# Attention units beside a projection: values, transposes and scores in one piece or in three

## The chip, the cores and the metric

The kernel runs on one core of a Trainium2 chip, as one program. The metric is the device time of an execution in microseconds, the median of several runs. Beside it there is one profiled execution, from which all durations come.

## What is computed

One decoder layer for a prompt of 1024 tokens and 8 single sampled tokens, all in fp32. The change lies in the prompt's attention, beside the input projection. The reference, cut to that:

```python
h = rms_norm(x, norm_mix_pre)
q, k, v, u, gates = jnp.split(h @ w_in, IN_SPLITS, axis=-1)
# three head groups of 4 heads x 64: (window, dilation) = (128,1), (512,4), (2048,16)
s = jnp.einsum('bnqrhd,bnkrhd->bnrhqk', qb, kw) * SCALE + bias
s = jnp.where(valid[None, :, None, None], s, NEG)
lse = jax.nn.logsumexp(s, axis=-1)
pr = jnp.exp(s - lse[..., None])
o = jnp.einsum('bnrhqk,bnkrhd->bnqrhd', pr, vw)
# the groups are combined with the softmax of their lse; then the attention output,
# a conformer convolution of u, gates, an output projection, a SwiGLU, an embedding
```

A block of 128 queries reads its own block of keys and, in the first group always but for the first block and in the second group for every other block, the block before. In the third group it reads its own block alone.

## The kernel before

**The projection.** The activations lie in SBUF with features on partitions, split into a high and a low part (`hh`, `hl`), as is each weight (`wh` on ScalarE, `wl` on VectorE, written by `ensure`). A bank of the projection (`gemm_bank`) is one PSUM bank of 384 or 264 tokens, into which 8 x 3 matmuls accumulate (L288 to L290: high x high, low x high, high x low). Each weight column block gives three banks, of 384, 384 and 264 tokens.

**The order of the work.** It is written out by hand in `CYCLES`: a triple (`triple(i)`: the q, k and v of two heads, 9 banks), then a pair (`u_pair`: gate and input of one block of the convolution, 6 banks), and so on, six of each. Then come the banks of the branch gates (`wi_gB`, `wi_gA`). After each bank `pump(BUD)` lets background generators go on, in their order: the depthwise convolution (30 operations of VectorE per block), the sampled tokens' attention, and `combine` with the layer norm. The program's instructions are then put in order for each engine by a scheduler that goes by this order and by what is ready, so that an instruction whose operand or buffer isn't free yet can be passed by later ones.

**A unit of attention** (`Unit`) is two query blocks of two heads (four blocks in the third group). It has three steps:

- `qk` (L645): scores of both heads into the PSUM banks `S0` and `S1`, from 64 rows each. VectorE adds the bias and takes the extreme, ScalarE exponentiates into two SBUF tiles `E`.
- `pt(i)` (L672): transposes of one half of the unit's `E`, 128x128 each, into the PSUM bank `PT`, and a copy by ScalarE to SBUF (`PTs`).
- `pv` (L690): values, `PTs` against the token-ordered v, into the PSUM bank `O`, 64 columns per head, and a copy by ScalarE to the output tile `oT`. After a triple's last unit `oT` is written to DRAM (`d_o`).

A triple of the first two groups has four units, one of the third two; there are 20 in all. They are queued when their triple's q, k and v are done (`triple_done`, after the first gate bank of the following pair) and run beside the banks that follow: `attn_slot` is called after each of the pair's three input banks, after each of the next triple's nine banks, and after the gate banks while units are left. When none is left there, `attn_done` gives the attention's PSUM banks to other work and queues `combine`.

**The slots before.** A unit takes two calls. In the first, `attn_slot` issues the values of the unit before and the scores of this one. In the second it issues `pt(0)` and leaves `pt(1)` in the list `mids`; the next bank calls it in its middle, ahead of its sixth of eight steps (`MID = 5`). So the projection is interrupted three times for each unit.

**The buffers in question.** `misc()` gives the next PSUM bank of a rotation; while units run it holds one bank alone, `m`. Other users of `m` there: the transpose of the sampled rows in `qkv_out` (L737), the first half of the transposes of v in `to_tok` (L764; the second half uses `PT`), and the transpose of the convolution's last rows (`rows`, L985), which runs at the end of the bank after a pair. The pool `sc` has four buffers, for `E`, `PTs` and the rows `nrow` and `zrow`. The pool `act` has 43 slots of 1032 columns, for q, k, v, outputs, split weights and the convolution's tiles.

Of the kernel before, what the change touches and what calls it, by code (L numbers as in the profile page):

```python
# [10 lines left out]
F32 = mybir.dt.float32  # L11
# [5 lines left out]
P = 128  # L17
# [41 lines left out]
def decoder_step(ctx: ExitStack, tc: tile.TileContext, ins, outs):  # L59
# [3 lines left out]
    def pool(name, bufs, space=None):  # L63
        if space is None:
            return ctx.enter_context(tc.tile_pool(name=name, bufs=bufs))
        return ctx.enter_context(tc.tile_pool(name=name, bufs=bufs, space=space))
# [9 lines left out]
    psa = pool("psa", 1, PSUM)  # L76
# [3 lines left out]
    def nm(s):  # L80
        uid[0] += 1
        return f"{s}_{uid[0]}"
# [4 lines left out]
    def sc(s, shape=(P, 512)):  # L87
        return scp.tile(list(shape), F32, tag="sc", name=nm(s))
# [14 lines left out]
    def misc():  # L103
        nonlocal mtags
        mtags.rotate(-1)
        return psa.tile([P, 512], F32, tag=mtags[-1], name=nm("m"))
# [185 lines left out]
    def gemm_bank(wi, xs, c, nk=KT, mid=None, at=MID):  # L292

        t0, n = rng(c)
        ps = bank()
        sp = W(wi)
        for k in range(nk):
            if k == at and mid is not None:
                mid()
            if k == MID and mids:  # L300
                mids.popleft()()
            xh, xl = xs[k]
            mm3(ps[:, :n], n, sp[0][:, k], sp[1][:, k],
                xh[:, t0:t0 + n], xl[:, t0:t0 + n], k == 0, k == nk - 1)
        while later:
            later.popleft()()
        return ps

    def gemm_bank_rows(wis, f, xs, c):

        t0, n = rng(c)
        ps = bank()
        nk = len(wis)
        for k in range(nk):
            xh, xl = xs[k]
            sp = W(wis[k])
            mm3(ps[:, :n], n, sp[0][:, f], sp[1][:, f],
                xh[:, t0:t0 + n], xl[:, t0:t0 + n], k == 0, k == nk - 1)
        return ps
# [104 lines left out]
    last = [j for j in range(NH) if all(j not in x for x in pairs)]  # L424
# [191 lines left out]
    class Unit:  # L616
# [46 lines left out]
                        A.activation(ev, ev, AF.Exp, scale=-1.0, bias=nm_, accum_out=l_)  # L663

        def pt(self, i):
            ps = psa.tile([P, 512], F32, tag="PT", name=nm("PT"))
            e, half = self.e[i], self.halves[i]
            for blk in half:
                for h in range(2):
                    for kb in range(0 if self.prev(blk) else 1, 2):  # L670
                        o = self.at(blk, h, kb)[1]
                        TE.transpose(ps[:, o:o + P], e[:, o:o + P], ident)  # L672
            self.p[i] = p = sc("PTs")
            if self.g == 2 or self.prev(half[0]):
                A.activation(p, ps, AF.Copy)
            else:
                A.activation(p.rearrange("p (h b q) -> p h b q", h=2, b=2)[:, :, 1],
                             ps.rearrange("p (h b q) -> p h b q", h=2, b=2)[:, :, 1], AF.Copy)
# [25 lines left out]
                    stats_by_tokens(g)  # L704

    steps = deque()
    flight = [None]
    mids = deque()

    def attn_slot():  # L710


        while mids:
            mids.popleft()()
        u = flight[0]
        if u is not None and u.p[0] is None:
            u.pt(0)
            mids.append(lambda: u.pt(1))
            return
        if u is not None:  # L720
            u.pv()
        flight[0] = steps.popleft() if steps else None
        if flight[0] is not None:
            flight[0].qk()

    def attn_busy():
        return bool(steps) or flight[0] is not None

    def attn_steps(g, hp, qT, kT, vtok, oT):
        steps.extend(Unit(g, hp, n, qT, kT, vtok, oT) for n in range(4 if g < 2 else 2))  # L730
# [269 lines left out]
    def u_pair(i):  # L1000
        sig, zs = {}, {}
        for c in range(3):
            ensure(wi_gate[i] + 1)
            u_banks(i, c, sig)
            if c == DONE and done:
                triple_done(done.pop())
            pump(BUD)
        for c in range(3):
            ensure(wi_a[i] + 1)
            a_banks(i, c, sig, zs)  # L1010
            attn_slot()
            pump(BUD)
# [73 lines left out]
    def triple(i):  # L1086
        for j in range(3):
            for c in (0, 2, 1) if i == 0 and j == 0 else range(3):
                ensure(wi_qkv[i, j] + 1)
                triple_bank(i, j, c)  # L1090
                attn_slot()
                pump(BUD)
        while attn_busy():
            attn_slot()
        done.append(i)
# [55 lines left out]
    for wis, dst in ((wi_gB, d_gB), (wi_gA, d_gA)):  # L1151
        for i in range(KT):
            for c in range(3):
                ensure(wis[i] + 1)
                t0, n = CH[c]
                ps = gemm_bank(wis[i], hs, c)
                s = rl("sg")
                A.activation(s[:, :n], ps[:, :n], AF.Sigmoid)
                SY.dma_start(dst[i, :, t0:t0 + n], s[:, :n])
                if attn_busy():  # L1160
                    attn_slot()
                elif rest:
                    rest.pop()()
                pump(BUD)
# [17 lines left out]
    for c in range(3):  # L1182
        t0, n = CH[c]
        for f in range(KT):
            ga = rl("ga")
            SY.dma_start(ga[:, :n], d_gA[f, :, t0:t0 + n])
            ps = gemm_bank_rows(wi_A, f, ohl, c)
# [675 lines left out]
```

## Time and profile before

| what | value |
|---|---|
| median of 3 runs | 1684.11 us (1683.31 to 1684.15) |
| profiled execution | 1686.02 us |
| its span, first to last instruction | 1684.2 us |
| mean granted clock of TensorE | 0.998 |
| TensorE matmuls busy | 1660.8 us, 99% of the span |
| VectorE busy | 1203.5 us, 71% |
| ScalarE busy | 670.2 us, 40% |
| GpSimd busy | 112.4 us, 7% |

How to read the rows of the profile: PE is TensorE's matmuls, PEld its weight loads, DVE is VectorE, ACT is ScalarE, POOL is GpSimd, SP issues transfers. A row of the timeline has the start in us from the span's start, the duration, engine, line, operation, output and inputs by name, the form (rows x columns of the array, then the moving operand) and the number of instructions merged. Matmuls overlap and their ends are modelled, so the time that one takes from the engine is read from start to start. L120 is the line of a helper through which all VectorE, ScalarE, GpSimd and SP instructions pass; those are told apart by their tiles. An fp32 matmul of scores or values appears as two instructions, a transpose as one. Rows of a waits view have the waiting instruction, what ended the wait, the sum in us, the number of times and the longest.

### The profile page before, as it was taken

Reading aid. Unit: us, or ns where it says so; the run is one execution under the profiler, and the core shown is the slowest. Engines: PE = TensorE matmul, PEld = TensorE weight load, DVE = VectorE, ACT = ScalarE, POOL = GpSimd, SP = SyncE. Lnnn points to the kernel's source line nnn. Section 1 sums busy time; section 2 is a strip of 40 time slices with the busy share of each in tenths; the row PEclk is TensorE's granted clock in tenths of the full one; section 3 lists DMA queues with packets and bytes.
Section 4 is the critical chain, followed back from the end, with each engine's and each line's share of the span. In section 5 each row is a group of like instructions: output and inputs, shape, how many; then the busy total and the mean of one; then the engine's idle time right before and its main releaser. Section 6 shows DMA issues by size and latency. Waiting matters only on the chain.

```text
span 1684.2 us, 29605 instructions
## 1 busy us (share of the span) xinstructions
PE 1660.8 (99%) x11843; PEld 1632.8 (97%) x11843; DVE 1203.5 (71%) x2156; ACT 670.2 (40%) x1419; POOL 112.4 (7%) x129
## 2 busy tenths in 40 slices
PE   7999999999999999999999999999999999999998
PEld 7999999999999999999999999999999999999998
DVE  7889879859979686644679666566678445668853
ACT  6434445444353345113445444344444341223520
POOL 1000000000000000000000000000000197200000
PEclk9999999999999999999999999999999999999999
DMA  5241121121355263522233245345445676740411
GB/s 192 65 126 61 49 68 39 55 90 56 102 163 171 85 192 121 160 81 87 92 116 113 97 164 187 140 176 201 169 150 194 238 253 229 254 143 14 156 54 47
DMA packets 103296, 217.00 MB, mean 129 GB/s; under 512 B 13074, under 2 KB 64098, under 8 KB 102774
## 3 DMA queue, kind: packets, MB, share of 16 engines
q1 hardware_dynamic: 102966, 214.97, 37.8%
q8 instruction: 93, 1.52, 0.4%
q0 software_dynamic: 192, 0.13, 0.1%
q14 instruction: 45, 0.37, 0.1%
HBM read 157.30 MB, written 71.26 MB: 136 GB/s over the span
## 4 chain that ended last, share of the span: by engine, by line
PE 91%; DVE 5%; ACT 1%; DMA 1%; issue 1%; POOL 0%; SPq 0%; POOLq 0%; DVEq 0%; ACTq 0%
PE g L288 29%; PE g L290 29%; PE g L289 29%; DVE y L120 3%; PE O L690 1%; PE S L645 1%; PE PT L672 1%; DVE wl L120 1%; DMA ux<-d_s 0%; PE m L347 0%; PE m L335 0%; DVE pk L120 0%; DMA strow<-in_state_conv_dram 0%; DVE ts L120 0%; DMA raw<-in_w_in_dram 0%
## 5 line engine op out<-in xcount | busy, mean ns | idle before, releaser
L288 PE MATMUL g<-hh,wh 128*128 128x384 f32 (+1 forms) x1200 | 393.5, 328 | 7.5 <-ACT wh L120 7.5
L290 PE MATMUL g<-hh,wl 128*128 128x384 f32 (+1 forms) x1200 | 384.8, 321 | 0.2 <-DVE wl L120 0.2
L289 PE MATMUL g<-hl,wh 128*128 128x384 f32 (+1 forms) x1200 | 384.3, 320 | 0.0
L120 DVE SCALAR_TENSOR_TENSOR y<-z,taps,y 128x1023 f32<-128x1023 f32 (+14 forms) x240 | 304.0, 1267 | 36.7 <-ACT y L120 31.1
L288 PEld LDWEIGHTS g<-hh,wh 128*128 128x128 f32 x1200 | 226.8, 189 | 14.8 <-ACT wh L120 7.5
L289 PEld LDWEIGHTS g<-hl,wh 128*128 128x128 f32 x1200 | 226.6, 189 | 0.6 <-DVE hl L120 0.3
L290 PEld LDWEIGHTS g<-hh,wl 128*128 128x128 f32 x1200 | 226.2, 188 | 0.8 <-DVE wl L120 0.8
L120 DVE TENSOR_TENSOR fa<-fa,g 128x258 f32<-128x258 f32 (+1 forms) x216 | 91.3, 433 | 84.2 <-PE g L290 72.7
L120 DVE TENSOR_TENSOR wl<-raw,wh 128x1024 fp32r<-128x1024 f32 x90 | 109.5, 1221 | 34.9 <-ACT wh L120 29.0
L288 PE MATMUL g<-mh,wh 128*128 128x344 f32 x336 | 108.0, 322 | 0.0
L290 PE MATMUL g<-mh,wl 128*128 128x344 f32 x336 | 107.4, 320 | 0.0
L289 PE MATMUL g<-ml,wh 128*128 128x344 f32 x336 | 107.3, 319 | 0.0
L120 ACT ACTIVATE wh<-raw 128x1024 fp32r<-128x1024 f32 x90 | 94.0, 1052 | 17.5 <-issue 7.7
L288 PE MATMUL g<-mh,wah 128*128 128x258 f32 x304 | 86.8, 287 | 5.5 <-DVE pk L120 5.5
L120 ACT ACTIVATE sg<-g 128x384 f32<-128x384 f32 (+1 forms) x68 | 31.0, 455 | 146.1 <-PE g L290 123.6
L289 PE MATMUL g<-ml,wah 128*128 128x258 f32 x304 | 87.0, 287 | 0.0
L290 PE MATMUL g<-mh,wal 128*128 128x258 f32 x304 | 86.9, 286 | 0.0
L288 PE MATMUL g<-th,wbh 128*128 128x258 f32 x304 | 86.4, 285 | 0.1
L289 PE MATMUL g<-tl,wbh 128*128 128x258 f32 x304 | 85.9, 283 | 0.0
L290 PE MATMUL g<-th,wbl 128*128 128x258 f32 x304 | 85.8, 283 | 0.0
L120 ACT ACTIVATE p<-g 128x258 f32<-128x258 f32 x114 | 42.6, 382 | 91.4 <-PE g L290 88.2
L120 DVE TENSOR_TENSOR acc<-acc,sq 128x344 f32<-128x344 f32 (+2 forms) x123 | 61.3, 512 | 17.6 <-ACT sq L120 15.2
(285 smaller groups left out, 4347.0 us busy)
## 6 DMA issues: line engine op xcount, KB each, us to landing
raw<-in_w_in_dram SPq DMA_DIRECT2D x50, 512.0 KB
raw<-in_w_ffn_in_dram SPq DMA_DIRECT2D x44, 512.0 KB
d_s<-tsh SPq DMA_DIRECT2D x16, 516.0 KB
d_s<-ts SPq DMA_DIRECT2D x16, 516.0 KB
ush<-d_s SPq DMA_DIRECT2D x16, 516.0 KB
usl<-d_s SPq DMA_DIRECT2D x16, 516.0 KB
raw<-in_w_ffn_out_dram SPq DMA_DIRECT2D x32, 256.0 KB
out_kvs_dram<-in_cache_kv_w_dram SPq DMA_DIRECT2D x16, 510.0 KB
```

The costliest lines, as they stand in the source:

```text
L120: ins = fn(*a, **k)
L288: TE.matmul(ps, hi_w, xh, start=first, stop=False, skip_group_check=more)
L289: TE.matmul(ps, hi_w, xl, start=False, stop=False, skip_group_check=more)
L290: TE.matmul(ps, lo_w, xh, start=False, stop=last, skip_group_check=more)
L645: TE.matmul(sp[h][:, o:o + nk], qT[h * 64:(h + 1) * 64, blk * P:(blk + 1) * P], kT[h * 64:(h + 1) * 64, (blk + 1) * P - nk:(blk + 1) * P], ...
L672: TE.transpose(ps[:, o:o + P], e[:, o:o + P], ident)
L690: TE.matmul(ps[h * 64:(h + 1) * 64, i * P:(i + 1) * P], vtok[:, k0:k0 + 64], self.p[half][:, o:o + P], start=kb == kbs[0], stop=kb == kbs[-1])
```

## The change

A unit now interrupts the projection once in every second call of `attn_slot`; the calls between return at once. In one piece it issues the values of unit k-1, both halves of the transposes of unit k and the scores of unit k+1. So a unit's scores, transposes and values lie two calls apart each, and three units are under way. The second half of the transposes takes its PSUM bank from `misc()` instead of `PT`. Nothing is put into `mids` any more.

```diff
         def pt(self, i):
-            ps = psa.tile([P, 512], F32, tag="PT", name=nm("PT"))
+            ps = psa.tile([P, 512], F32, tag="PT", name=nm("PT")) if i == 0 else misc()
             e, half = self.e[i], self.halves[i]
...
     steps = deque()
-    flight = [None]
+    flight = [None, None]
     mids = deque()
+    turn = [0]
 
     def attn_slot():
 
 
-        while mids:
-            mids.popleft()()
-        u = flight[0]
-        if u is not None and u.p[0] is None:
+        turn[0] ^= 1
+        if not turn[0]:
+            return
+        last, u = flight
+        if last is not None:
+            last.pv()
+        if u is not None:
             u.pt(0)
-            mids.append(lambda: u.pt(1))
-            return
-        if u is not None:
-            u.pv()
-        flight[0] = steps.popleft() if steps else None
-        if flight[0] is not None:
-            flight[0].qk()
+            u.pt(1)
+        flight[:] = u, steps.popleft() if steps else None
+        if flight[1] is not None:
+            flight[1].qk()
 
     def attn_busy():
-        return bool(steps) or flight[0] is not None
+        return bool(steps) or any(u is not None for u in flight)
```

By the count of calls, twelve from one `triple_done` to the next, a triple's four units begin at the second call and end at the twelfth, where before they began at the first and ended at the ninth.

## The prediction

> **What bounds the kernel now.** I read the page first, its chain above all, then the busy times of the stretch in which attention runs, then the matmuls of TensorE one by one around single interruptions, and last the waits.
>
> ```profile
> span 1684.2 us, 29605 instructions
> ...
> PE 91%; DVE 5%; ACT 1%; DMA 1%; issue 1%; POOL 0%; SPq 0%; POOLq 0%; DVEq 0%; ACTq 0%
> ```
>
> The chain that ended last runs on TensorE for 91% of 1684.2 us. The units of attention lie between 100 and 480 us, and there the busy times are:
>
> ```profile
> 100.00:480.00 380.00, 379.71 (x2664) 361.46 (x2664) 329.11 (x462) 172.99 (x420) 4.60 (x6) 1.00 0.21 68
> ```
>
> TensorE is busy for 379.71 of 380.00 us, VectorE for 329.11 and ScalarE for 172.99, at full clock. So in this stretch what TensorE gains or loses is gained or lost by the kernel one for one, and a latency elsewhere counts only where TensorE comes to wait for it. The profiled execution took 1686.02 us, its span plus 1.8 us around it, and the runs have a median of 1684.11. I make the sum as a difference in the profiled execution and add it to the median.
>
> The question is what one interruption costs, beyond the matmuls that it must do anyway. I time it by starts: from the last projection matmul before to the second one after, less the usual step of these two.
>
> ```profile
> 213.38 0.34 PE L289 MATMUL g<-hl,wh 128*128 128x384 f32 x1
> 213.56 0.34 PE L290 MATMUL g<-hh,wl 128*128 128x384 f32 x1
> 213.73 0.60 PE L672 MATMUL PT<-ident,E 128*128 128x128 f32 x4
> 214.09 0.42 PE L288 MATMUL g<-hh,wh 128*128 128x384 f32 x1
> 214.34 0.34 PE L289 MATMUL g<-hl,wh 128*128 128x384 f32 x1
> ```
>
> A 384-wide matmul is followed by the next after 0.175 us (213.38 to 213.56). Four transposes: 214.34 - 213.56 - 2 x 0.175 = 0.43 us, 0.11 each. The third row starts at the usual step after the one before. The first matmul behind it is lengthened, to 0.25, but this is inside the 0.43. Scores and values are another matter:
>
> ```profile
> 254.98 0.34 PE L290 MATMUL g<-hh,wl 128*128 128x384 f32 x1
> 255.25 0.93 PE L645 MATMUL S<-kT,qT 64*128 64x128 f32 x8
> 256.10 0.45 PE L288 MATMUL g<-hh,wh 128*128 128x384 f32 x1
> 256.38 0.34 PE L289 MATMUL g<-hl,wh 128*128 128x384 f32 x1
> ```
>
> ```profile
> 294.02 0.29 PE L289 MATMUL g<-hl,wh 128*128 128x264 f32 x1
> 294.14 0.28 PE L290 MATMUL g<-hh,wl 128*128 128x264 f32 x1
> 294.35 0.88 PE L690 MATMUL O<-PTs,vtok 128*64 128x128 f32 x12
> 295.16 0.44 PE L288 MATMUL g<-hh,wh 128*128 128x384 f32 x1
> 295.44 0.34 PE L289 MATMUL g<-hl,wh 128*128 128x384 f32 x1
> ```
>
> ```profile
> 284.49 0.34 PE L290 MATMUL g<-hh,wl 128*128 128x384 f32 x1
> 284.75 0.88 PE L690 MATMUL O<-PTs,vtok 128*64 128x128 f32 x12
> 285.56 0.93 PE L645 MATMUL S<-kT,qT 64*128 64x128 f32 x8
> 286.42 0.44 PE L288 MATMUL g<-hh,wh 128*128 128x384 f32 x1
> 286.69 0.34 PE L289 MATMUL g<-hl,wh 128*128 128x384 f32 x1
> ```
>
> Scores alone cost 256.38 - 254.98 - 0.35 = 1.05. Both are of the second head group, the same size as in the third fence. Values alone cost 295.44 - 294.14 - 0.12 - 0.175 = 1.00, the step of a 264-wide matmul being 0.12 (294.02 to 294.14). Both in one piece cost 286.69 - 284.49 - 0.35 = 1.85, so 0.20 us less than apart. Where the form changes from 128*128 to 64*128 or 128*64 the next start comes late: 255.25 is 0.27 after 254.98, 0.09 over the step, and the second matmul behind the piece comes after 0.28, 0.10 over it. Transposes have the form of the projection, 128*128, and show no late start in front of them. This is the whole argument: what costs is not the interruption but the change of form, and the transposes don't change it.
>
> **The change part by part.**
>
> *Interruptions removed.* Two per unit, both made of transposes alone. At 0.43 us for four they cost the transposes' own 0.11 each and nothing besides, at a bank's end or in the middle of a bank. Taking them out of the projection saves 0.00 us; the same transposes are issued.
>
> *Transposes between values and scores.* Before, a triple of four units had the pieces S0, O0+S1, O1+S2, O2+S3, O3, with transposes in between. After, it has S0, T0+S1, O0+T1+S2, O1+T2+S3, O2+T3, O3. A triple of two units had S0, O0+S1, O1 and gets S0, T0+S1, O0+T1, O1. Values and scores stood side by side at 4 x 3 + 2 x 1 = 14 places, and after the change at none. The trace of before doesn't show transposes next to either. If they act there as the projection does, being of its form, each of the 14 places loses the 0.20: +2.8 us. If both borders of the transposes cost no more than the border of values and scores, the 14 borders O to T and the 14 borders T to S save 0.20 each against a pass over the projection, and the balance is -28 x 0.20 + 14 x 0.20 = -2.8 us. I take a value near the upper end, since the nearest row to a transpose is the projection's, the same 128*128. Part of the late start of scores (0.09) can run within the last transpose's 0.11, of which its 128 columns need not take all: I count a third, 0.03 x 14 = 0.4 off. That gives +2.4 us.
>
> The Trainium skill, page "TensorEngine Tiling (Array Packing)", section Key Properties, says that changing the tiling mode, and not just the tile, drains TensorE. It speaks against this change: O to T to S holds two changes of mode where O to S holds one. The trace agrees: late starts stand at the changes of form and nowhere else. By this rule alone each of the 14 pieces has one drain more and the sum lies above zero; the page has no figure for the drain.
>
> *Waits for the exponentials go.* Before, the transposes come one bank behind the scores; after, two.
>
> ```profile
> 396.49 0.34 PE L290 MATMUL g<-hh,wl 128*128 128x384 f32 x1
> 396.67 1.19 PE L672 MATMUL PT<-ident,E 128*128 128x128 f32 x4
> 397.61 0.37 PE L288 MATMUL g<-hh,wh 128*128 128x264 f32 x1
> 397.82 0.28 PE L289 MATMUL g<-hl,wh 128*128 128x264 f32 x1
> ```
>
> ```profile
> PEld PT L672 <- ACT E L120: 1.2, 5, 0.2
> PEld g L290 <- DVE wl L120: 1.1, 3, 0.8
> ```
>
> Here four transposes cost 397.82 - 396.49 - 0.175 - 0.12 = 1.03, 0.60 over their price: VectorE, deep in the convolution, was late with the softmax's maxima. The weight loader's waits for E add up to 1.2 us in five pieces, and a little more on the array: I take -1.3 us. What is late next is nothing on TensorE: the transposes come a bank later still, 24 x 0.12 = 2.9 us at least. If VectorE's delay grows as much, the 1.3 stay: bounds -1.3 to 0.
>
> *The second half's bank.* pt(1) writes "m" in place of "PT", so the two halves don't wait for each other's copy. Elsewhere this costs nothing; at the first unit of each triple "m" is just in use (second rival).
>
> *Held longer.* q and k of a triple live one bank longer, its token-ordered v and its output three. The 43 slots also hold split weights; VectorE's waits row above shows only 1.1 us of waiting for a weight's low part, so there is room now (third rival). The four "sc" buffers hold P of one unit and E of the next between two pieces, all four; each is released in the piece that needs it again, so no new wait: the values come first there.
>
> *Later end.* The last values come three gate banks later, 2 x 24 x 0.175 + 2.9 = 11.3 us, and with them attn_done and the write of d_o. The first scores of the last triple's second unit fall among sigmoids, which costs ScalarE two more table loads; it has more than half its time free. The cover of the end:
>
> ```profile
> L288 PE MATMUL g<-oh,wh x48: 282/335/446, 657.5 to 681.4; 128*128 128x384 f32 x32, 128*128 128x264 f32 x16
> ...
> L120 DVE TENSOR_TENSOR ol<-ogl,oh x2: 1232/1233/1234, 610.2 to 618.3; 128x1032 fp32r<-128x1032 f32 x2
> ```
>
> The combined heads are ready at 618.3 + 1.2 and first used at 657.5, 38 us later; the 11.3 lie inside. Without that cover they would be the cost. So 0.
>
> **Sum:** +2.4 - 1.3 = +1.1 us: 1687.1 in the profiled execution, **1685.2** as a median. A measurement of this kernel tells about 0.2%, 3.4 us, from no change, so this is "no change".
>
> **The rivals.**
>
> *1. Faster: borders inside a piece are free.* For it: all of a piece is attention's own plain fp32 and O to S is cheap. Against it: the row of 128*128. Its price is the lower end, -2.8 - 1.3 = -4.1: 1680.0.
>
> *2. Slower: pt(1) waits for "m".* At the first bank of the triple's stage the transpose of a convolution's tail goes to "m" right in front of T0.
>
> ```profile
> 200.26 0.27 PE L985 MATMUL m<-ident,t 128*38 128x128 f32 x1
> 200.37 0.60 PE L672 MATMUL PT<-ident,E 128*128 128x128 f32 x4
> ```
>
> ```profile
> 201.12 0.32 ACT L120 ACTIVATE zrow<-m 38x128 f32<-38x128 f32 x1
> ```
>
> ScalarE has read "m" at 201.44. Were pt(1) queued straight behind pt(0), at 200.37 + 0.43 = 200.80, TensorE would stand for 0.64 us, with the scores and the next bank's matmuls queued behind it; six triples make 3.8 us, and 1.1 + 3.8 = +4.9: 1689.0. It decides from 0.4 us per triple on. Against it:
>
> ```profile
> 242.82 0.27 PE L737 MATMUL m<-ident,samp 128*24 128x128 f32 x1
> 242.93 0.60 PE L764 MATMUL m<-ident,vT 128*128 128x128 f32 x4
> ...
> 244.95 0.60 PE L764 MATMUL m<-ident,vT 128*128 128x128 f32 x4
> ```
>
> ```profile
> 243.40 0.25 ACT L120 ACTIVATE nrow<-m 24x128 f32<-24x128 f32 x1
> ```
>
> The same case in to_tok: its first half goes to "m" while "m" is still to be read (at 243.40), so the four that start at 242.93 without a wait are the second half, in "PT", and the first half was put nine matmuls later, at 244.95. The program's order is by readiness. I expect the same: at six of 20 units pt(1) is moved behind the scores into the next bank, so the change doesn't do there what it says. Transposes cost the same there, so the sum stands.
>
> *3. Slower: slots.* With q, k, v and outputs held longer, weight splits come later until TensorE waits. For it: E, weights, convolution rows and heads share one pool. Against it: a weight's two slots come free with each weight finished. One us per triple would add 6: 1691.2.
>
> **How the numbers follow.** My forecast has 0.66, the first rival 0.12, the second 0.14, the third 0.08. The forecast's own range goes from 1.9 - 1.3 (twice the 0.03 off at each border) to 2.8 - 0 (no discount, no wait gone): 1684.7 to 1686.9. The range for 8 in 10 takes in most of the second rival and the edge of the first: 1680.8 to 1689.7. Faster by over 0.2% (below 1680.7): 0.10 of the first rival and 0.02 of the forecast, 0.12. Slower (above 1687.5): 0.14 of the second and 0.06 of the third, 0.20. The same: the rest, 0.68.
>
> **What would show it.** Right: a piece of values, eight transposes and scores costs 0.12 to 0.20 us more than the sum of values with scores and 8 x 0.11; its first transpose comes late, as the projection does after values; the waits of transposes for E are gone from the loader's rows; pt(1) of six units stands some matmuls inside a bank; TensorE's busy time between 100 and 480 us stays whole. Wrong: borders without late starts (first rival), idle TensorE before transposes with ScalarE's zrow as releaser (second), matmuls that wait for wh or wl (third).

## The result, and the profile after

| what | before | after |
|---|---|---|
| median | 1684.13 us (6 runs, 1682.39 to 1685.53) | 1693.43 us (6 runs, 1690.99 to 1696.19) |
| profiled execution | 1686.02 us | 1692.18 us |
| its span | 1684.2 us | 1690.0 us |
| mean granted clock of TensorE | 0.998 | 0.998 |

The ratio is 1.0051, interval 1.0038 to 1.0063: slower by 9.3 us. The forecast was no change, 1685.2, and the range ended at 1689.7. L645, L672 and L690 keep their numbers; behind them the lines are one higher (L985 is L986, L843 is L844, L876 is L877).

The page of after, its span and its chain:

```profile
span 1690.0 us, 29607 instructions
...
PE 93%; DVE 3%; DMA 2%; issue 1%; ACT 1%; POOL 0%; SPq 0%; POOLq 0%; ACTq 0%; DVEq 0%
```

The stretch of attention in the windows view of after (the busy us of PE, PEld, DVE, ACT and POOL, each with its count, then the granted clock, the DMA share and GB/s):

```profile
100.00:480.00 380.00, 379.40 (x2617) 359.25 (x2616) 323.20 (x456) 168.98 (x416) 2.56 (x3) 1.00 0.19 62
```

TensorE is as busy as before (379.40 against 379.71 of 380.00). The busy time does not show the loss: TensorE does less in it, 2617 recorded matmuls for 2664. What shows it is the price of a piece, taken from start to start as in the prediction. Here are all pieces summed between the same two projection matmuls, at 111.2 and 544.4 us before, at 109.8 and 549.9 us after:

| pieces | before | after |
|---|---|---|
| transposes alone | 34: 14.72 | |
| convolution row, transposes | 6: 2.85 | |
| values, scores | 14: 29.03 | |
| first pieces: row, transposes, scores | | 6: 16.16 |
| values, transposes, scores | | 8: 23.46 |
| values, transposes | | 6: 11.42 |
| scores alone, values alone, work on v | 22: 18.62 | 22: 18.62 |
| sampled tokens' attention | 3: 1.38 | 3: 3.54 |
| sum | 66.59 | 73.21 |

The time between the two matmuls grew from 433.23 to 440.10, by 6.87: 4.44 in attention's own pieces, 2.16 in the sampled tokens' attention, 0.26 in the projection itself and rounding. The spans differ by less, 5.74, because the profiled execution of before came to the first of the two matmuls 1.4 us later, in the start-up, where the matmuls come in the same order in both.

The first loss, in the timeline of TensorE of after, at the second triple's first piece (start, duration, line, tiles, form, count):

```profile
197.30 0.34 PE L290 MATMUL g<-hh,wl 128*128 128x384 f32 x1
197.47 0.27 PE L986 MATMUL m<-ident,t 128*38 128x128 f32 x1
197.58 0.38 PE L672 MATMUL PT<-ident,E 128*128 128x128 f32 x2
197.89 0.70 PE L645 MATMUL S<-kT,qT 64*128 64x256 f32 x2
198.68 0.66 PE L672 MATMUL m<-ident,E 128*128 128x128 f32 x4
199.26 1.13 PE L645 MATMUL S<-kT,qT 64*128 64x256 f32 x6
200.32 0.44 PE L288 MATMUL g<-hh,wh 128*128 128x384 f32 x1
200.60 0.34 PE L289 MATMUL g<-hl,wh 128*128 128x384 f32 x1
```

`pt(1)`, the four transposes to `m`, has neither waited behind `pt(0)` nor gone to the next bank. It stands inside the scores, two instructions behind their start. This piece costs 200.60 - 197.30 - 0.35 = 2.95 us. In five of the six triples the scores are cut up in some such way. In the fifth all eight transposes stand together ahead of the scores, and the second four start 0.43 us after the first four instead of 0.11: there pt(1) waits for `m`, as the second rival had it. The waits of TensorE and of its weight loader at these transposes have a new row each:

```profile
PE m L672 <- ACT zrow L120: 0.4, 2, 0.3
```

```profile
PEld m L672 <- ACT zrow L120: 1.8, 5, 0.5
```

The loader's waits for E, 1.2 us before, have no row any more.

The second loss, in the timeline of TensorE of after, behind the last triple:

```profile
498.30 0.34 PE L288 MATMUL g<-hh,wh 128*128 128x384 f32 x1
499.63 0.27 PE L844 MATMUL m<-ident,smx 128*4 128x128 f32 x1 [1.00 <-DVE smx L120]
...
520.71 0.28 PE L288 MATMUL g<-hh,wh 128*128 128x264 f32 x1
521.71 0.39 PE L877 MATMUL m<-cc,sacc 128*128 128x8 f32 x2 [0.72 <-DVE sacc L120]
```

A transpose and small products of the sampled tokens' attention stand here in TensorE's order, and TensorE is idle in front of them for 1.00 and 0.72 us, until VectorE has made `smx` and `sacc`. The same place before:

```profile
490.31 0.34 PE L290 MATMUL g<-hh,wl 128*128 128x384 f32 x1
490.48 0.27 PE L843 MATMUL m<-ident,smx 128*4 128x128 f32 x1
490.51 0.37 PE L288 MATMUL g<-hh,wh 128*128 128x264 f32 x1
```

```profile
L120 DVE TENSOR_REDUCE smx<-score x1: 265/265/265, 489.7 to 489.7; 128x4 f32<-128x64 f32 x1
```

The last row, from the view of the tile `smx` (least, median and longest ns, then the start), says that VectorE's reduction started at 489.7 and took 0.27: `smx` was ready half a microsecond ahead. The reason for the delay stands in SP's timeline, first before, then after:

```profile
450.01 0.37 SPq L120 DMA_DIRECT2D raw<-in_w_in_dram  x1
450.49 0.36 SPq L120 DMA_DIRECT2D sq<-d_qkv  x1
```

```profile
483.19 0.38 SPq L120 DMA_DIRECT2D sq<-d_qkv  x1
```

The sampled tokens' loads are issued 33 us later.

### The profile page after: what moved, and what is told of

Same layout as the page of the kernel before. It is cut to its first block, busy times and chain, and to the rows that moved or that the text cites. A ratio compares the mean times of both kernels' runs of the same rounds, so it can differ in the third digit from the quotient of the medians.

```text
span 1690.0 us, 29607 instructions
## 1 busy us (share of the span) xinstructions
PE 1665.7 (99%) x11843; PEld 1634.5 (97%) x11843; DVE 1203.8 (71%) x2156; ACT 673.9 (40%) x1423; POOL 112.5 (7%) x129
## 4 chain that ended last, share of the span: by engine, by line
PE 93%; DVE 3%; DMA 2%; issue 1%; ACT 1%; POOL 0%; SPq 0%; POOLq 0%; ACTq 0%; DVEq 0%
PE g L288 30%; PE g L290 29%; PE g L289 29%; PE S L645 1%; PE O L690 1%; DMA skv<-in_cache_kv_w_dram 1%; PE m L672 1%; PE PT L672 0%; DMA ux<-d_s 0%; DVE skv L120 0%; DVE sacc L120 0%; PE m L347 0%; PE m L335 0%; DVE pk L120 0%; DVE ts L120 0%
```

## The experiments

My theory after the two traces had two losses, the cut-up first pieces (3.9 us) and the last triple's late end (2.2 us), beside changes of form of about the size forecast. The rivals were that one of the two is the whole, and that the order values, transposes, scores is what costs. All ratios are to the kernel before, measured again beside each. A kernel with several edits is named by them.

**The changed kernel again** (nothing edited).

> The changed kernel once more, beside the others, to settle how much there is to explain. Its profiled execution lies 6.2 us over that of before (5.7 in the span), its median 9.3 over the median. If the profiled execution is the typical one, the median is now 6 to 7.5 us over before; if something that comes and goes (loads, the granted clock) adds 3 us in most executions, it is again 9 us over, and the granted clock or the wait for the sampled tokens' loads is worse than before in this profile.

Measured: 1692.73 us beside 1684.87, ratio 1.0050, interval 1.0036 to 1.0064: 7.9 us. Attention's pieces are the same to 0.01 us. Yet this profiled execution has a span of 1693.8 us, 3.8 over the other one of the same kernel. Its windows around the small products:

```profile
522.00:524.60 2.60, 1.57 (x12) 1.57 (x13) 2.60 (x5) 0.09 (x1) 0.00 (x0) 1.00 0.00 0
524.60:528.00 3.40, 3.40 (x13) 3.40 (x12) 3.40 (x5) 1.25 (x2) 0.00 (x0) 0.50 0.22 58
```

TensorE was idle for 1.25 us in front of the small products, and the granted clock then was 0.50 for 3.4 us; 13 matmuls were done in this time. In the first profiled execution the idle time was 0.72, and the same stretch had full clock and 21 matmuls:

```profile
520.80:523.30 2.50, 1.78 (x15) 1.59 (x13) 2.50 (x5) 0.10 (x1) 0.00 (x0) 1.00 0.00 0
523.30:526.70 3.40, 3.40 (x21) 3.40 (x21) 3.40 (x5) 1.24 (x2) 0.00 (x0) 1.00 0.19 60
```

So the late end has a price that comes and goes: between the two matmuls of the table this execution took 442.14 us, 2.0 more, of which 0.6 are longer waits and 1.5 the projection at half clock. How much of the medians (9.3 and 7.9, above the 6.9 of the first profile) comes from it can be read from the mean granted clock, which is on record for every execution: 0.9976 on average in the 11 of the changed kernel, 0.9979 in 57 of the kernel before. As an estimate, 0.0002 of 1690 us is 0.4 us. So it is a small part of the difference. The 6.9 itself lies inside both intervals, 6.4 to 10.6 us and 6.1 to 10.8.

**The bank `O` for the first units' second half.** In the piece of a triple's first unit there are no values, so `O` is free.

```diff
-            ps = psa.tile([P, 512], F32, tag="PT", name=nm("PT")) if i == 0 else misc()
+            if i and self.n:
+                ps = misc()
+            else:
+                ps = psa.tile([P, 512], F32, tag="O" if i else "PT", name=nm("PT"))
```

> The changed kernel, with one edit: in the first unit of a triple, where there are no values in the piece, the second half of the transposes takes the bank O (free there) and not m. Theory A (half of the loss comes from pt(1) being put inside the scores at the six first units, since m is still to be read by zrow): the first pieces become eight transposes (four in the last two triples' groups as they come), then the scores in one run, and cost what 8 x 0.11 and scores alone cost; the 0.76, 0.93, 0.70, 0.59, 0.37 and 0.56 us by which they were above that go, 3.9 us, and the time falls from 1693.4 to about 1689.5, 0.23%. Theory B (the loss is in what is held longer and comes late, the sampled tokens' attention and its loads): the pieces become cheaper by at most some tenths and the time stays at 1693.4 within 1 us, since the waits near 484 to 523 us take it back. Theory C (the loss is the order values, transposes, scores as such): no change either, and the first pieces keep their cost.

Measured: 1687.15 us beside 1684.94, ratio 1.0015, interval 1.0006 to 1.0024: 2.3 us less than theory A's 1689.5, which started from the median 1693.4. Between the two matmuls of the table this kernel takes 2.65 us more than the kernel before, inside the interval (1.0 to 4.0 us). The same piece in the timeline of this kernel:

```profile
197.44 0.34 PE L290 MATMUL g<-hh,wl 128*128 128x384 f32 x1
197.62 0.27 PE L989 MATMUL m<-ident,t 128*38 128x128 f32 x1
197.73 0.82 PE L675 MATMUL PT<-ident,E 128*128 128x128 f32 x6
198.48 1.14 PE L645 MATMUL S<-kT,qT 64*128 64x256 f32 x8
199.54 0.44 PE L288 MATMUL g<-hh,wh 128*128 128x384 f32 x1
199.82 0.34 PE L289 MATMUL g<-hl,wh 128*128 128x384 f32 x1
```

It costs 199.82 - 197.44 - 0.35 = 2.03, for 2.95. The six first pieces sum up to 12.24 us for 16.16: 3.92 us, as theory A had it, and nothing else among the pieces moved by more than 0.24. The rows say where the 0.93 of this piece went: eight score instructions in one run take 199.54 - 198.48 = 1.06, 0.27 for two. Cut up, the first two take 198.68 - 197.89 = 0.79, the four transposes 0.58 for 0.44, the last six 1.06 for 0.80: 0.52, 0.14 and 0.26 more. How the scores start says what this is made of. Windows of the timeline that end 0.3 us behind the first score, of this kernel and of the changed one, show how many have begun by then:

```profile
198.48 0.49 PE L645 MATMUL S<-kT,qT 64*128 64x256 f32 x2
```

```profile
197.89 0.48 PE L645 MATMUL S<-kT,qT 64*128 64x256 f32 x1
```

In one run the eight go in four pairs, an instruction of each head's 64 rows, 0.01 us apart, and the next pair 0.2 to 0.3 us later. Cut up, the first two start 0.32 apart and the last two 0.22, each alone, so eight instructions take six places in place of four: the two places more, about 0.22 each, are 0.43 of the 0.93. Another 0.16 is the wait for `zrow`: here the transposes start 0.46 behind the last score ahead of them; in the first triple, where they don't wait, 0.31. That leaves some 0.3 for the changes of form, an estimate. Over the six triples the wait is 0.16 + 0.36 + 0.03 + 0.32 = 0.9 us of the 3.9, the 0.32 in the fifth, where nothing is cut up. This edit removes the greater part of the change's loss.

**The last triple by the old pattern.** The old function stays beside the new one.

```diff
+    def attn_slot():
+        (slot_joined if (newest[0] == 5) == False else slot_apart)()
...
+        newest[0], turn[0] = i, 1
```

> The changed kernel, but the sixth and last triple's units go by the old pattern (three interruptions per unit, pt(1) in PT); the first five triples stay as changed. Theory A: the last triple's late end costs 2.2 us in the stretch from 484 to 523 us (the sampled attention's loads are issued at 483 us in place of 450, and TensorE waits for it in its order); that goes, with 0.56 us of the last triple's first piece, and up to 0.8 us of waits for E come back: 1693.4 - 2.0 to 2.8 = 1690.6 to 1691.4. If the 3 us by which the medians differ more than the profiled executions (9.3 against 5.7) come from those loads as well, then 1687.6 to 1688.4. Theory B (all of the loss is in the pieces, and the waits at the end are only where it shows): one sixth of it goes, 1.5 us, 1691.9, and the waits near 484 to 523 us remain.

Measured: 1690.93 us, ratio 1.0036, interval 1.0022 to 1.0050: 1.8 to 2.5 us less than the two medians of the changed kernel, though the intervals overlap. The loads are back at 454 us, the waits at `smx` and `sacc` are gone and the sampled pieces cost 1.37 again. That is theory A; by theory B they would have remained. One new wait took some of it back, that of the last triple's transposes for `PT`, until ScalarE had copied it:

```profile
PE PT L672 <- ACT PTs L120: 0.6, 1, 0.6
```

**Only the last triple by the new pattern**, in the kernel before: the same functions with `== True`.

> The kernel before, with the new pattern for the sixth triple alone. Theory A: the sampled attention's loads are issued about 30 us later, TensorE waits 2.2 us in 484 to 523 us, the triple's first piece costs 0.56 more, and up to 0.8 of waits for E goes: 1684.1 + 2.0 to 2.8 = 1686.1 to 1686.9, and up to 1689.9 if the 3 us that the medians show beyond the profiles hang on those loads. Theory B (the pieces are the whole, evenly over the triples): the triple has two units of the 20, one first piece of six and no piece of values, transposes and scores; +0.6 - 0.8 = about no change, 1683.9 to 1684.7.

Measured: 1687.98 us (11 runs, 1686.56 to 1692.09) beside 1684.94, ratio 1.0020, interval 1.0011 to 1.0029: 3.0 us, a little over theory A's first figure (2.0 to 2.8) and far from theory B's. One triple of six, with two of the 20 units, brings a third of the loss. Its waits of TensorE:

```profile
PE m L867 <- DVE smx L120: 1.1, 1, 1.1
PE m L900 <- DVE sacc L120: 0.8, 1, 0.8
```

The loads are issued at 479 us here, with five triples as before. So it is the last triple's pattern alone that delays them.

**Transposes ahead of the values.**

```diff
-        if last is not None:
-            last.pv()
         if u is not None:
             u.pt(0)
             u.pt(1)
+        if last is not None:
+            last.pv()
```

> The changed kernel, with the transposes ahead of the values in a piece: transposes, values, scores. If the price of a piece goes by its changes of form between 128*128 and another (my reading: values and scores side by side save 0.20, transposes beside the projection cost nothing), the eight pieces with all three lose the 0.15 each, 1.2 us, and the six pieces with transposes and values alone gain or lose nothing but the 0.05 that they showed: 1693.4 - 0.9 to 1.2 = 1692.2 to 1692.5, too little for the times but plain in the pieces' prices. Rival (values behind transposes wait for nothing, but transposes now come ahead of the values and their E one piece's length earlier, so the buffers of sc, released by the values in the same piece, come free later than PTs needs them): TensorE waits in front of the values or in the next piece's transposes, 0.5 us and more per piece, eight pieces, +4 us and more.

Measured: 1690.23 us, ratio 1.0033, interval 1.0020 to 1.0045: 2 us below what either reading gave. A full piece in the changed kernel:

```profile
289.31 0.34 PE L290 MATMUL g<-hh,wl 128*128 128x384 f32 x1
289.58 0.88 PE L690 MATMUL O<-PTs,vtok 128*64 128x128 f32 x12
290.39 0.44 PE L672 MATMUL PT<-ident,E 128*128 128x128 f32 x2
290.66 0.60 PE L672 MATMUL m<-ident,E 128*128 128x128 f32 x4
291.19 0.93 PE L645 MATMUL S<-kT,qT 64*128 64x128 f32 x8
292.05 0.39 PE L288 MATMUL g<-hh,wh 128*128 128x264 f32 x1
292.27 0.28 PE L289 MATMUL g<-hl,wh 128*128 128x264 f32 x1
```

The same one with the transposes first:

```profile
289.00 0.34 PE L290 MATMUL g<-hh,wl 128*128 128x384 f32 x1
289.18 0.38 PE L672 MATMUL PT<-ident,E 128*128 128x128 f32 x2
289.40 0.60 PE L672 MATMUL m<-ident,E 128*128 128x128 f32 x4
289.93 0.88 PE L690 MATMUL O<-PTs,vtok 128*64 128x128 f32 x12
290.73 0.93 PE L645 MATMUL S<-kT,qT 64*128 64x128 f32 x8
291.59 0.39 PE L288 MATMUL g<-hh,wh 128*128 128x264 f32 x1
291.81 0.29 PE L289 MATMUL g<-hl,wh 128*128 128x264 f32 x1
```

They cost 2.66 and 2.51. The second is values with scores (1.86) and six transposes at 0.11, so beside the projection transposes cost only themselves. Where the 0.15 goes is seen at the borders. Values start 0.27 after the last projection matmul, transposes 0.18: 0.09. Two transposes behind values take 0.27 to the next start, behind the projection 0.22: 0.05. The four behind them take 0.53 whether values or scores come next. All eight such pieces gained, 23.46 to 22.28, 0.15 each; the six of values and transposes lost 0.04 each, 11.42 to 11.69. That is the first reading's 0.9, and no wait of the rival's came. In the medians it was 2.5 to 3.2 us. What the pieces don't account for lies partly in the sampled pieces, 2.44 for 3.54: the shifted order happened to reach `smx` without a wait.

**Three edits together:** bank `O`, transposes first, the last triple by the old pattern.

> The changed kernel with three edits together: the bank O for the first units' second half (6.3 us faster alone in the medians, 3.9 in the pieces), the old pattern for the last triple (2.5 us faster alone), transposes ahead of values (3.2 us faster alone in the medians, 1.0 in the pieces). If these add up by the pieces and waits: the time of the kernel before + 7 - 3.4 - 2.2 - 1.0 = about before + 0.5, with the waits for E at four fifths of the pieces gone and those of the last triple back, so 1684 to 1685.5. If the sums of the medians held (6.3 + 2.5 + 3.2 = 12 us), it would be 3 us faster than before.

Measured: 1685.31 us beside 1684.87, ratio 1.0000, interval 0.9991 to 1.0009. The pieces sum up to 66.81 us, before 66.59. With both losses mended, the change, now in five of the six triples, is worth nothing, as the sum by pieces had it; the sum of the medians is refuted.

**The sampled tokens' instructions later**, in the changed kernel:

```diff
         V.tensor_reduce(mx, score.rearrange("p s h -> p h s"), axis=AX.X, op=ALU.max)
+        yield 3.0
+        yield 3.0
...
-        yield 3.0
-        yield 3.0
+        for _ in range(4):
+            yield 3.0
```

> The changed kernel; only, the sampled tokens' attention gives TensorE its two transposes two banks later and its last small products two banks later than now (more yields ahead of them), so that TensorE's queue doesn't reach them before the late operands. Theory A (the last triple's late end makes the sampled tokens' loads late, and TensorE stands in its queue in front of those instructions): the idle TensorE at L844 and L877, 1.0 and 0.7 to 0.9 us and the weight loads behind them, goes, 2.2 us in all: 1693.4 to 1691.2; the loads themselves stay as late as they are. Rival (VectorE's late work itself is what costs, whatever TensorE's order is: it holds the slots of the weights of the next banks): the wait only moves to the weights' low parts or to combine, and the time stays within 0.7 us.

Measured: 1696.75 us, ratio 1.0073, interval 1.0060 to 1.0086, 3.3 to 4.0 us more than the changed kernel, where theory A had 2.2 us less and the rival no change: both times missed. At its own place theory A held: no wait at `smx` or `sacc`, sampled pieces 1.42, the time between the two matmuls 437.94 for 440.10. But the wait came back, as the rival had it though larger, 150 us later:

```profile
669.41 0.69 PE L288 MATMUL g<-oh,wh 128*128 128x384 f32 x1 [4.49 <-DVE mA L120]
```

The layer norm runs together with `combine`, which is queued behind the sampled tokens. With four more banks of delay VectorE still had layer norm to do when TensorE had filled its PSUM banks with the first products of the combined heads, and TensorE stood until one was emptied into `mA`. The stall was again followed by half clock:

```profile
669.20:672.60 3.40, 3.19 (x10) 3.19 (x11) 3.40 (x9) 3.40 (x10) 0.00 (x0) 0.50 0.81 256
```

**The same with bank `O` and transposes first.**

> The changed kernel with the bank O for the first units' second half, the transposes ahead of the values, and the sampled tokens' transposes and products two banks later; the last triple stays in the new pattern. Theory A: the pieces cost what the same work costs apart, the 1.5 us of waits for E stay gone, the sampled attention's 2.2 us go: before - 1.5 to before - 0.5, 1683.2 to 1684.4. If the rival of the run before holds (VectorE's late work costs by itself), 2 us more, 1685.5 to 1686.5.

Measured: 1691.37 us beside 1684.87, ratio 1.0040, interval 1.0027 to 1.0053. Both theories missed. Between the two matmuls it took 433.04 us, 0.2 less than before, and from there to 690 us it lost 6.4 us in the same way, half clock included.

**Bank `O` and transposes first, the last triple at its first, third, fourth and fifth call.**

```diff
+    plan = deque()
...
-        if not turn[0]:
+        if not (plan.popleft() if plan else turn[0]):
             return
...
         if i == 5:
+            plan.extend((1, 0, 1, 1, 1))
             bg.append(sample_attention())
```

> The changed kernel with the bank O for the first units' second half, transposes ahead of values, and the last triple's four pieces at its first, third, fourth and fifth call, so that it begins and ends at the calls of the kernel before. My theory after the runs so far (the loss is the split scores, the two borders of transposes, and the last triple's late end; the gain is the E waits): all three losses are gone and the 1.5 us of E waits stay gone, since the first transposes come two banks after their scores: before - 1.5, within 1 us, and the sampled tokens' loads are issued near 450 us again without a wait at the two transposes and the products. Rival (the slots held by q, k, v and outputs longer in the five other triples cost by themselves): the loads stay near 480 us, or waits for weights appear, and the time is before + 1 or more.

Measured: 1686.37 us beside 1684.71, ratio 1.0009, interval 1.0000 to 1.0018. A miss: the triple ends at the call where it ended before, but the loads were still issued late, at 474 us, and TensorE stood 1.0 us in front of `smx`. SP's timeline of this kernel shows what stands just ahead of them:

```profile
473.49 0.39 SPq L120 DMA_DIRECT2D out_cvp_dram<-zrow  x1
473.93 0.30 SPq L120 DMA_DIRECT2D out_cvs_dram<-zrow  x1
474.32 0.35 SPq L120 DMA_DIRECT2D sq<-d_qkv  x1
```

In the kernel before, as shown above, the load of a weight stands there. With the new pattern in the last triple, early or late, the loads come in SP's order behind the writes of the convolution's rows, which wait for `zrow` of the last convolution's bank; with the old pattern, ahead of them. So the end of the last values alone doesn't decide: with it back in its place, 9 of the 33 us went (474 us, for 483 in the changed kernel). That the loads' slots of `act` were expected free later, so that they were put further back, is my reading; no run took the slots apart from the order.

**Bank `O` and transposes first alone.**

> The changed kernel with the bank O and transposes ahead of values, the last triple late as in the change: what it is over before is the last triple's late end alone. By the pieces: -1.5 for E waits, 0 for the pieces, +2.2 for the sampled attention, and 1.7 more where a stretch of 3.4 us at half clock follows TensorE's stall, as it did in one of the two profiled executions of the changed kernel: before + 0.7 to + 2.4, 1685.6 to 1687.3. Rival (the end costs nothing by itself): before - 1.5.

Measured: 1685.37 us beside 1684.71, ratio 1.0006, interval 0.9997 to 1.0015, at the low end of what was expected (+0.7 to +2.4); 1.5 us faster, the rival's, lies outside the interval. The pieces without the sampled ones sum up to 64.84 us, before 65.21; the sampled ones cost 2.54 for 1.38. My expectation had the right total with a wrong term: the pieces did not come to 0 but to +1.2 beside the E waits (64.84 - 65.21 + 1.54), since six scores that stood behind values now stand behind transposes alone.

## Why the prediction was wrong

**Interruptions removed, 0.00: right.** Transposes beside the projection cost 0.11 each inside a joint piece as alone, as the kernel with transposes first shows.

**Transposes between values and scores, +2.4: right in kind, a little large.** By the pieces it is 8 x 0.15 for values, transposes, scores; 6 x 0.20 for the first pieces, whose scores have lost the values beside them; and -0.3 for the six of values and transposes: +2.1. The two changes of form, O to T and T to S, together cost 0.15 more than O to S, inside the bounds, and nearer to the upper one as the row of 128*128 said. The first rival is out.

**Waits for the exponentials, -1.3: right.** The 34 pieces of transposes cost 14.72 us where 26 x 0.44 + 8 x 0.22 = 13.2 is their price without waits; the 1.5 are gone.

**The second half's bank, 0: the step that failed.** The prediction said that "at six of 20 units pt(1) is moved behind the scores into the next bank" and "Transposes cost the same there". In five of the six triples the scheduler moved it, but only into the middle of the scores; in the fifth it didn't move it and pt(1) waited. It cost 3.9 us, shown by the kernel with bank `O`. That the place goes by when `m` was expected to be free is my reading of it. The row from `to_tok` proved that the order goes by readiness. It didn't prove where a moved piece lands: in `to_tok` the neighbours were projection matmuls of the same form, which can be parted for nothing; here they were scores, of another form and going in pairs, which cannot. The second rival named the place, the tile and nearly the sum (3.8), but by another mechanism, a plain wait; by the starts that wait makes up 0.9 us of it.

**Held longer, 0: right for the weights,** for which TensorE got no new wait.

**Later end, 0: the second failure.** The cover that it named, 38 us of the combined heads, belongs to `combine`. In front of `combine` the same list holds the sampled tokens' attention, and its instructions on TensorE had 0.5 us of cover. It cost 2.2 us, and 1.5 more where half clock followed; the old pattern in the last triple removes the 2.2 and the new pattern there alone brings them. What came late wasn't the end itself but the sampled tokens' loads, which moved further back in SP's order, a queue that the prediction didn't look at for this step. The 38 us were no cover either: after four banks more of delay the layer norm beside `combine` was late by 4.5 us. The prediction followed one tile to its use, where a shift moves everything queued behind it.

The terms as measured, +2.1 - 1.5 + 3.9 + 2.2 + 0.2 in the projection itself, make the 6.9 us of the profiles. The medians are 1.0 and 2.4 higher, which their intervals allow; by the recorded clocks half clock is only a small part of that, and whether there is anything else stays open. The other kernels whose loss lies between the same two matmuls fit as well: bank `O` +2.65 us there against the kernel before, the last triple old +5.53, it alone new +2.03, transposes first +4.87, three edits +0.48, and the last two +0.86 and +1.00, each inside the interval of its executions.

No kernel beat the one before. The E waits, 1.5 us, are all that this change was seen to win, and the changes of form take most of them back: 1.2 us in the last kernel.

## What to carry to other kernels

Work whose operand or buffer isn't ready is not simply late: look at what the scheduler will put it between, since the same four transposes cost nothing extra among matmuls of their own form and up to 0.9 us among scores, whose pairs they parted. If a generator or a queue ends later, check the first user of everything behind it in the same list, and count as cover the smallest slack among them, not that of the tile one thought of. Busy time can't show such losses; prices from start to start can.

## What the runs showed of the hardware

Idle times of TensorE of 1.25 us (the changed kernel again), 4.49 and 4.44 us (the two kernels with the sampled tokens later) were followed by half clock or ended in it, a granted clock of 0.50 for 3.4 us and, in the last of them, 6.8 us; those of 0.72, 0.87 and 1.1 us were not. It is not the length alone. Every kernel here, the one before too, is idle for 2.7 us near 1210 us and again near 1255 us, waiting for VectorE's `pk`. All 12 profiled executions had half clock after the second, and only 8 after the first. Of the four without (bank `O`, the last triple alone, and the last two), three were 1.7 to 2.0 us faster than the kernel before between 1190 and 1300 us; the fourth had 6.8 us of half clock after the second. So spans of single executions differ by as much as the effects looked for here, and the stretch between two matmuls is the better measure.

The Trainium skill, page "TensorE: Matmul & The Clock Gate", section "What's actually happening", has half rate come after at least one idle window of about 3.4 us. The slow stretches here last 3.4 us or twice that; but 2.7 us of idle time brought one in 20 of 24 cases and 1.25 us in one, so a short stall can cost 1.5 us beside itself.
